# The last row tile's products in two half banks, and the first output-gate load behind the rows

## The chip, the cores and the metric

One core of a Trainium2 chip runs the kernel. The metric is the device time of one execution in microseconds, the median of several executions. The engines are named as in the profile: PE (TensorE, matrix products; PEld is its weight load), DVE (VectorE), ACT (ScalarE), POOL (GpSimd) and SP (SyncE, which here issues most of the DMAs). An engine works through its own instructions in order, and semaphores tie the engines together.

## The reference, cut to what matters

One decoder layer over 16 learned meta tokens and 1,024 rows of width 1,024, all in float32:

```python
u = rmsnorm(h, mix_norm_pre)
q, f_logit, i_in, g_out, v_pool, gate_a, gate_b = split(u @ w_in)
a = hgrn2(q, f_logit, i_in, g_out, ...)      # gated recurrence, 4 heads of 128
p = multiscale_pool(v_pool, pool_proj, pool_scale)
z = sigmoid(gate_a) * (a @ w_branch_hgrn) + sigmoid(gate_b) * (p @ w_branch_pool)
h = h + rmsnorm(z @ w_out, mix_norm_post)
u = rmsnorm(h, ffn_norm_pre)
gt = causal_dwconv(u @ ffn_w_gate, ffn_conv_w, ffn_conv_b)
y = (gelu(gt) * (u @ ffn_w_up)) @ ffn_w_down     # inner width 2,816
h = h + rmsnorm(y, ffn_norm_post)
return h[:, 16:]
```

`rmsnorm` divides each row by the root of its mean square and multiplies by a gain. The change touches three places: the loads at the very start (for the first `u @ w_in`), two scratch tiles in `hgrn2`, and the last product with its norm and row sum.

## The kernel before

**Precision.** Each float32 operand is split into a high and a low part of the type that PE multiplies at full rate, and a product is three: high by high, high by low, low by high (`mm3`, lines 187 to 190). So one block of 128 rows, one step of k and 512 columns is three matmuls of 512 columns into one PSUM bank (2 KB per partition, 512 floats; there are eight).

**The start.** `load_row` (line 451) issues the DMA of a tile of 128 rows on SP; `load_wi` (line 457) those of the weights of the value projection. In the text the order is: row tile 0, the gain, value weights 0, row tile 1, value weights 1 to 3, the other row tiles, small parameters. Then come, in an order written out by hand for PE, ACT and DVE (`manual_schedule`): 14 warm-up products of the identity (`warm`), the norm of a row tile (square on ACT with a sum per row, root, reciprocal and scaling on DVE), its transposes on PE into `pt` (line 431), the split into `uhi` and `ulo` (lines 434 and 436), the split of the value weights (lines 516 and 517), and the products `pv`. SP and POOL are not in that list. Their instructions, like all instructions outside such blocks, are ordered by a planner at build time, which lets an instruction go ahead as soon as what it needs is there. `Loader` (line 168) issues the DMAs of the next weights and their split through `wsplit` (line 149; its DMA is line 151, its cast line 154, its subtraction 155). At the end of the value projection a `Loader` is made for the first two output-gate projections ("G", line 1106), the first user of its buffers.

**The heads.** `head_steps` (line 646) runs one head of the recurrence in pieces that alternate with other products. It takes two scratch tiles: `sc` (128 by 1,024, the score matrix, zeroed by POOL at line 657) and `near` (128 by 256, the scores close to the diagonal, zeroed at line 658, two buffers for four heads). The products of six levels are written into them: into `near` by a predicated copy on DVE (line 720), into `sc` by plain copies (line 714); at the end `near` is copied into `sc` (line 777).

**The tail.** The last product of the layer is computed by a scheme with seven products of half size instead of eight (Strassen's), over four row tiles of 128 (NT = 4) in each half of the rows and 512 columns in each half of the columns. Its partial results stand in the SBUF tiles `c11`, `c12`, `c21` and `c22` (arrays named `acc` in the profile). Three of its stages run with both halves, eight banks at a time (`pa`, `pb`); `leave` adds them to the tiles. The last stage, from line 1759 on, has four banks, one for each tile. Over five steps of k (6 to 10) the products of all four tiles alternate with finishing the lower half of the rows; then each of the four upper tiles gets its last six steps of k and is finished:

- line 1777: DVE subtracts `c11` from the bank,
- `half_norm` (line 1699): ACT squares the 512 columns with a sum per row (1701), DVE multiplies them in place by the gain `g4` (1702),
- `finish` (line 1706): ACT takes the root (1708), DVE the reciprocal (1710) and, for each half of the columns, product and row sum (1714), and SP stores it (1715).

The right half of the columns, `c12`, has been through `half_norm` by then. `prep_last` splits operands for the last two steps of k. The order of the tail's instructions from line 1759 on is the planner's.

Of the kernel before, what the change touches and what calls it, by code (L numbers as in the profile page):

```python
# [11 lines left out]
AF = mybir.ActivationFunctionType  # L12
# [30 lines left out]
KT = 6  # L43
# [28 lines left out]
def trunk_kernel(ctx: ExitStack, tc: tile.TileContext, x, meta_tokens, mix_norm_pre,  # L72
# [35 lines left out]
    def bank(name="ps"):  # L108
        return stage["ps", "p"].tile([P, 512], F32, tag="ps", name=nm(name))
# [341 lines left out]
    def load_row(t0, rows):  # L451
        row = slot(D, name="row")
        src = meta_tokens[:, :] if t0 == 0 else x[0, t0 - NM : t0 - NM + rows, :]
        nc.sync.dma_start(row[:rows], src)
        return row

    def load_wi(j):
        raw = slot(1024, name="wiraw")
# [187 lines left out]
    def head_steps(h):  # L646
# [8 lines left out]
        near = small([P, NCH * SB], "near", "near", 2)  # L655
        n3 = near.rearrange("p (c t) -> p c t", c=NCH)
        pool_e.memset(sc, 0.0)
        pool_e.memset(near, 0.0)

        def over(t):  # L660
            return t[:, :NM].rearrange("p (o t) -> p o t", o=1).to_broadcast([P, HALO, NM])
# [254 lines left out]
    def job(kind, i):  # L916
        if kind == "F":
            return (wblock(WIN, 0, KD, CF + i * P, P), KD, u_all, CH_ALL, lambda r: post_f(i, r))
        if kind == "Q":
            return (wblock(WIN, 0, KD, CQ + i * P, P), KD, u_q, CH_Q, lambda r: post_q(i, r))  # L920
        if kind == "G":
            return (wblock(WIN, 0, KD, CG + i * P, P), KD, u_q, CH_Q, lambda r: post_g(i, r))
        if kind == "PV":
            return (wblock(WIN, 0, KD, CV + i * P, P), KD, u_all, CH_ALL, lambda r: post_pv(i, r))
        if kind == "PP":
            return (pool_proj[0, i].rearrange("(k c) d -> c k d", k=1), 1,
                    lambda k, lo, n: (pin[i][0][:, lo : lo + n], pin[i][1][:, lo : lo + n]), CH_Q,
                    lambda r: post_pp(i, r))
        if kind == "BA":
            return (wblock(w_branch_hgrn[0], 0, HEADS, i * P, P), HEADS, a_x, CH_Q, lambda r: post_branch(sas, i, r))  # L930
        return (wblock(w_branch_pool[0], 0, HEADS, i * P, P), HEADS, p_x, CH_Q, lambda r: post_branch(sbs, i, r))
# [122 lines left out]
    with tc.manual_schedule(engines={E.Activation, E.DVE, E.PE}):  # L1054
        warm(14)
        n0, n1 = (norm_steps(rows_in[i], P, g1) for i in range(2))
        next(n0)
        next(n0)
        un0 = next(n0)
        f0 = feature_steps(un0, P, uhi, ulo, vtiles[0][0])  # L1060
        split_wi(raws[0])
        next(f0)
        next(f0)
        next(f0)
        next(n1)
        next(f0)
        next(n1)
        un1 = next(n1)
        v_mm(vb[0], vtiles[0][0], 0)
        v_mm(vb[0], vtiles[0][0], 1)  # L1070
        split_wi(raws[1])
        f1 = feature_steps(un1, P, uhi, ulo, vtiles[1][0])
        next(f1)
        next(f1)
        split_wi(raws[2])
        next(f1)
        next(f1)
        split_wi(raws[3])
        for i, j in ((0, 1), (1, 0), (0, 2), (1, 1), (0, 3), (1, 2), (1, 3)):
            for k in (2 * j, 2 * j + 1):  # L1080
                v_mm(vb[i], vtiles[i][0], k)
        v_norm(2)
        v_norm(3)
        for i in range(2):
            v_feat(2 + i)
            v_norm(4 + i)
        for i in range(2):
            v_out(vb[i], vtiles[i][0])
        for i in range(2, len(vtiles)):
            ps = bank("pv")  # L1090
            for k in range(KD):
                v_mm(ps, vtiles[i][0], k)
            if i < 5:
                v_feat(i + 2)
            if i == 5:
                v_feat(7)
                v_feat(8)
            v_norm(i + 4)
            if i == 3:
                params()  # L1100
            if i == 5:
                for q in ("t2", "t1", "t3", "t4"):
                    two_halves(gq, q)
                sums = [gate_steps(d) for d in ds]
            if i == len(vtiles) - 1:
                gl = Loader([job("G", h)[:2] + (P,) for h in range(EARLY_G)])
            for j in SUMS_AT.get(i, ()):
                next(sums[j], None)
            v_out(ps, vtiles[i][0])
        gates.load_first(0)  # L1110
        gates.load_first(1)
        gates.ahead(2)
        for h in range(EARLY_G):
            src, n_k, xs, chunks, post = job("G", h)
            r = proj(None, 0, n_k, xs, chunks, ws=gl.next(), name="pg", by_bank=2 * h)
            if h == EARLY_G - 1:
                post(r)
            for j in SUMS_AT.get(9 + 2 * h, ()):
                next(sums[j], None)
            if h < EARLY_G - 1:  # L1120
                post(r)
            if h == 0:
                dve.tensor_tensor(vm_hl[:NM], vm_hl[:NM], vm_low[:NM], ALU.add)
                nc.sync.dma_start(vmd, vm_hl[:NM])
                gates.load_first(2)
                gates.ahead(4)
            for j in SUMS_AT.get(10 + 2 * h, ()):
                next(sums[j], None)

        close_pool("ps")  # L1130
        open_pool("pf", 4, PSUM)
        gates.load_first(3)
        for e in range(0, EARLY, 2):
            p = gates.start_pair(e)
            for f in [f[i] for i in range(2) for f in p]:
                f()
                for j in SUMS_AT.get(13, ()) if e == 0 else ():
                    next(sums[j], None)
# [532 lines left out]
    def prep_last(k, hold):  # L1671

        load_ops(3, k)
        if hold:
            hi, lo = slot(1024, F32R, "yh"), slot(1024, F32R, "yl")
        else:
            i = next_rot()
            hi, lo = big[1][:, i, :], big[1][:, 2 + i, :]
        cut(hi, lo, loads.pop((3, k)))
        held[k] = (hi[:, :512], lo[:, :512]), (hi[:, 512:], lo[:, 512:])  # L1680
# [76 lines left out]


    banks = [bank("pd") for _ in range(NT)]
    for n, k in enumerate(range(KT, KH)):  # L1760
        if n == 0:
            prep_last(KH - 2, False)
            for t in range(NT):
                dve.tensor_tensor(c12[t], c12[t], pb[t], ALU.add)
            prep_last(KH - 1, False)
        multiply(banks, held.pop(k), n == 0, False)
        if n < NT:
            half_norm(c22[n], NT + n, 1)
            half_norm(c21[n], NT + n, 0)
            finish(NT + n, c21[n], c22[n])  # L1770
            load_h(n)
        if n > 0:
            half_norm(c12[n - 1], n - 1, 1)
    for t in range(NT):
        for j in range(KT):
            multiply(banks, held[j], False, j == KT - 1, [t])
        dve.tensor_tensor(c11[t], banks[t], c11[t], ALU.subtract)
        half_norm(c11[t], t, 0)
        finish(t, c11[t], c12[t])
    close_pool("ps", "sm", "fm")  # L1780


# [27 lines left out]
```

## Time and profile before

| | us |
|---|---|
| time, median of 3 runs | 1331.35 (1329.1 to 1331.79) |
| the profiled execution | 1331.5 |
| its span, from the first instruction to the last | 1329.8 |
| PE busy | 1302.7 |
| DVE, ACT, POOL busy | 968.0, 572.9, 438.5 |

In the profile a line such as "L1777 DVE TENSOR_TENSOR acc<-pd,acc 128x512" is one instruction or a group: line of the program, engine, operation, what it writes and what it reads. A view in order of time begins with the start and the duration in us; brackets tell how long the engine stood idle before it and what ended that. Durations of one engine's instructions overlap somewhat, since an instruction starts while the one ahead is still writing. PE's matmuls overlap more: each is shown with its whole passage, and the pace is the distance of their starts. In a view of groups come the count, the total in us and the mean in ns. "SPq" marks the issue of a DMA; the data land later.

### The profile page before, as it was taken

The numbers are of one execution on the slowest core, as the hardware profiler recorded it, in microseconds if no ns is written. First come the engines' busy times: TensorE is split into PE (matmuls) and PEld (weight loads), VectorE is DVE, ScalarE is ACT, GpSimd is POOL, SyncE is SP. The second block draws the span as 40 slices with busy tenths as digits, with TensorE's granted clock in tenths as the row PEclk, the third lists the DMA queues.
The fourth block names the chain that finished last, engine by engine and source line by source line (L and its number), as shares of the span: only waits on it lengthen the run. The fifth ranks groups of instructions, "written<-read, shape, count | busy, mean of one in ns | idle before, by whom it ended". The sixth has DMA issues, their size and how long they took to land.

```text
span 1329.8 us, 21860 instructions
## 1 busy us (share of the span) xinstructions
PE 1302.7 (98%) x8665; PEld 1159.9 (87%) x8665; DVE 968.0 (73%) x1229; ACT 572.9 (43%) x962; POOL 438.5 (33%) x333
## 2 busy tenths in 40 slices
PE   8999999998899999999999999999999999999997
PEld 6799899998898999987899888888888888888886
DVE  5765655379967767766678999888999895455757
ACT  5553333366666665235564222322222233444443
POOL 2015331226624710051025555545555652000000
PEclk9999999998998999999999999999999999999999
DMA  7134533321011157987686777676766799666644
GB/s 260 53 105 145 134 111 104 108 69 49 19 52 36 35 175 263 337 287 253 229 291 231 192 207 193 196 206 164 181 157 141 183 237 318 216 224 222 222 174 158
DMA packets 139832, 230.56 MB, mean 173 GB/s; under 512 B 9080, under 2 KB 77340, under 8 KB 139730
## 3 DMA queue, kind: packets, MB, share of 16 engines
q1 hardware_dynamic: 127666, 204.78, 45.9%
q0 software_dynamic: 12064, 24.38, 11.1%
q8 instruction: 68, 1.11, 0.3%
q14 instruction: 34, 0.28, 0.1%
HBM read 165.59 MB, written 86.57 MB: 190 GB/s over the span
## 4 chain that ended last, share of the span: by engine, by line
PE 91%; DVE 3%; ACT 2%; DMA 2%; issue 1%; POOL 1%; SPq 0%; DVEq 0%; ACTq 0%
PE P L311 15%; PE P L312 15%; PE P L314 15%; PE pd L188 5%; PE pd L190 5%; PE pd L189 5%; PE pm L188 2%; PE pm L190 2%; PE pm L189 2%; PE ppv L208 1%; PE ppv L212 1%; PE ppv L209 1%; PE pbb L208 1%; PE pbb L209 1%; PE pbb L212 1%; PE pv L189 1%
## 5 line engine op out<-in xcount | busy, mean ns | idle before, releaser
L312 PE MATMUL P<-v,whi 128*128 128x512 f32 (+2 forms) x408 | 140.7, 353 | 0.0
L311 PE MATMUL P<-v,whi 128*128 128x512 f32 (+2 forms) x408 | 140.7, 352 | 0.0
L314 PE MATMUL P<-v,wlo 128*128 128x512 f32 (+2 forms) x424 | 135.1, 349 | 0.0
L1544 DVE TENSOR_TENSOR rot<-wraw,rot 128x1024 fp32r<-128x1024 f32 x31 | 37.9, 1224 | 72.3 <-ACT rot L1543 72.3
L282 POOL TENSOR_TENSOR swa<-wraw,wraw 128x512 f32<-128x512 f32 x28 | 43.4, 1549 | 138.9 <-DMA wraw<-in_ffn_w_gate_dram 73.9
L311 PEld LDWEIGHTS P<-v,whi 128*128 128x128 f32 x408 | 76.7, 188 | 10.5
L312 PEld LDWEIGHTS P<-v,whi 128*128 128x128 f32 x408 | 76.6, 188 | 10.2
L314 PEld LDWEIGHTS P<-v,wlo 128*128 128x128 f32 x424 | 74.0, 188 | 10.8
L256 ACT CAST whi<-wraw 128x512 fp32r<-128x512 f32 x78 | 46.1, 617 | 86.5 <-PE P L312 63.0
L190 PE MATMUL pd<-rot 128*128 128x512 f32 x272 | 82.1, 389 | 0.0
L189 PE MATMUL pd<-rot 128*128 128x512 f32 x272 | 82.1, 389 | 0.0
L188 PE MATMUL pd<-rot 128*128 128x512 f32 x272 | 81.1, 389 | 0.1
L1543 ACT CAST rot<-wraw 128x1024 fp32r<-128x1024 f32 x31 | 32.7, 1054 | 90.8 <-PE pd L190 89.4
L257 DVE TENSOR_TENSOR wlo<-wraw,whi 128x512 fp32r<-128x512 f32 x74 | 65.9, 912 | 2.8 <-ACT whi L256 2.7
L256 ACT CAST whi<-swa 128x512 fp32r<-128x512 f32 x56 | 33.4, 619 | 79.2 <-PE P L312 76.4
L1472 DVE SCALAR_TENSOR_TENSOR y<-g,par,y 128x1024 f32<-128x1024 f32 x44 | 65.6, 1491 | 0.8
L257 DVE TENSOR_TENSOR wlo<-swb,whi 128x512 fp32r<-128x512 f32 x56 | 61.4, 1102 | 6.0 <-ACT whi L256 6.0
L256 ACT CAST whi<-swb 128x512 fp32r<-128x512 f32 x56 | 33.4, 619 | 69.8 <-PE P L312 65.4
L188 PEld LDWEIGHTS pd<-rot 128*128 128x128 f32 x272 | 51.1, 188 | 11.1 <-DVE p L1480 0.5
L189 PEld LDWEIGHTS pd<-rot 128*128 128x128 f32 x272 | 51.0, 188 | 10.6
L190 PEld LDWEIGHTS pd<-rot 128*128 128x128 f32 x272 | 51.0, 188 | 10.6
L311 PE MATMUL P<-t4h,whi 128*128 128x258 f32 (+1 forms) x196 | 57.0, 307 | 0.0
(426 smaller groups left out, 4096.0 us busy)
## 6 DMA issues: line engine op xcount, KB each, us to landing
wraw<-in_w_in_dram SPq DMA_DIRECT2D x36, 512.0 KB, 5.1
yt<-ysum SPq DMA_DIRECT2D x33, 512.0 KB, 5.4
wraw<-in_ffn_w_gate_dram SPq DMA_DIRECT2D x26, 512.0 KB, 6.4
wraw<-in_ffn_w_up_dram SPq DMA_DIRECT2D x22, 512.0 KB, 5.9
wsum<-in_ffn_w_down_dram SPq DMA_DIRECT2D x22, 512.0 KB, 9.1
wraw<-in_w_out_dram SPq DMA_DIRECT2D x18, 512.0 KB, 4.8
ysum<-ys SPq DMA_DIRECT2D x11, 768.0 KB, 6.8
sa<-sscr SPq DMA_DIRECT2D x16, 513.0 KB, 6.4
```

The lines of the kernel that those rows point to most:

```text
L188: pe.matmul(ps, ahi, bhi, start=first, stop=False)
L189: pe.matmul(ps, ahi, blo, start=False, stop=False)
L190: pe.matmul(ps, alo, bhi, start=False, stop=last)
L256: act.copy(hi, src)
L257: (pool_e if 4 <= i < 2 * self.early else dve).tensor_tensor(lo, src, rr(hi), ALU.subtract)
L282: pool_e.tensor_tensor(s1, a21, a22, ALU.add)
L311: pe.matmul(d, whi[:, k, :], xh[:, c : c + w], start=(k == 0 and onto is None), stop=False, **go)
L312: pe.matmul(d, whi[:, k, :], xl[:, c : c + w], start=False, stop=False, **go)
L314: pe.matmul(x[:, o : o + w], wlo[:, k, :], xh[:, c : c + w], start=False, stop=(k == 3), **go)
L1472: dve.scalar_tensor_tensor(a, g[:, j : j + SEQ], cvw[:, j, m : m + 1], a, ALU.mult, ALU.add)
L1543: act.copy(hi, src)
L1544: dve.tensor_tensor(lo, src, rr(hi), ALU.subtract)
```

## The change

Three edits.

- The DMAs of the first two output-gate weights are queued on SP behind the DMA of the last row tile (`issue_after`: order of issue alone, with no wait for landing).
- `near` is no longer zeroed by a memset. It is copied on POOL from the first 256 columns of `sc`, just zeroed. So it can't run ahead of that memset, whose tile comes free later.
- In the last stage the fourth row tile's products are made in two pieces of 256 columns, in two banks: the one that it had, and a fifth (a bank that `pb` used; the addition of `pb[0]` to `c12[0]` is written ahead of `prep_last` for that). After the other three tiles are finished, the left piece gets its last six steps of k, then the right one. Each piece is subtracted, squared and multiplied by the gain on its own, the product into a new tile `left` and not in place; the left piece's sum of squares is added to the bias of the root by one small DVE instruction. Then `finish` follows as before.

```diff
     def load_row(t0, rows):
         row = slot(D, name="row")
         src = meta_tokens[:, :] if t0 == 0 else x[0, t0 - NM : t0 - NM + rows, :]
-        nc.sync.dma_start(row[:rows], src)
+        loaded_row.append(nc.sync.dma_start(row[:rows], src))
         return row
+
+    loaded_row = []
...
         pool_e.memset(sc, 0.0)
-        pool_e.memset(near, 0.0)
+        pool_e.tensor_copy(near, sc[:, : NCH * SB])
...
             if i == len(vtiles) - 1:
-                gl = Loader([job("G", h)[:2] + (P,) for h in range(EARLY_G)])
+                with tc.issue_after(loaded_row[-1].ins):
+                    gl = Loader([job("G", h)[:2] + (P,) for h in range(EARLY_G)])
...
     banks = [bank("pd") for _ in range(NT)]
+    pieces = [(banks[-1], slice(0, 256)), (bank("pd"), slice(256, 512))]
+
+    def multiply_pieces(ops, first, last, which=pieces):
+        (yh, yl), (wh, wl) = ops
+        tt = slice((NT - 1) * P, NT * P)
+        for ps, n in which:
+            mm3(ps[:, :256], (yh[:, tt], yl[:, tt]), (wh[:, n], wl[:, n]), first, last)
+
     for n, k in enumerate(range(KT, KH)):
         if n == 0:
+            dve.tensor_tensor(c12[0], c12[0], pb[0], ALU.add)
             prep_last(KH - 2, False)
-            for t in range(NT):
+            for t in range(1, NT):
                 dve.tensor_tensor(c12[t], c12[t], pb[t], ALU.add)
             prep_last(KH - 1, False)
-        multiply(banks, held.pop(k), n == 0, False)
+        ops = held.pop(k)
+        multiply(banks, ops, n == 0, False, range(NT - 1))
+        multiply_pieces(ops, n == 0, False)
...
-    for t in range(NT):
+    for t in range(NT - 1):
         for j in range(KT):
             multiply(banks, held[j], False, j == KT - 1, [t])
         dve.tensor_tensor(c11[t], banks[t], c11[t], ALU.subtract)
         half_norm(c11[t], t, 0)
         finish(t, c11[t], c12[t])
+    t = NT - 1
+    left = slot(512, name="left")
+    sums4 = small([P, 1], "sums4", "mq", 6)
+    for i in range(2):
+        ps, n = pieces[i]
+        for j in range(KT):
+            multiply_pieces(held[j], False, j == KT - 1, pieces[i : i + 1])
+        dve.tensor_tensor(c11[t][:, n], ps[:, :256], c11[t][:, n], ALU.subtract)
+        act.activation(junk[:, n], c11[t][:, n], AF.Square, accum_out=ssq4[:, 0, t : t + 1] if i else sums4)
+        dve.tensor_tensor(left[:, n], c11[t][:, n], g4[:, n], ALU.mult)
+        if i == 0:
+            dve.scalar_tensor_tensor(ssq4[:, 1, t : t + 1], sums4, 1.0 / D, ssq4[:, 1, t : t + 1],
+                                     ALU.mult, ALU.add)
+    finish(t, left, c12[t])
```

## The prediction

> **What bounds the kernel now.** I read the page first, then the busy time of each engine in five stretches, then the two ends in order of time, because the first view says that only the ends and one stretch in the middle have anything to give.
>
> ```profile
> span 1329.8 us, 21860 instructions
> ...
> PE 91%; DVE 3%; ACT 2%; DMA 2%; issue 1%; POOL 1%; SPq 0%; DVEq 0%; ACTq 0%
> ```
>
> ```profile
> 0.00:17.00 17.00, 11.37 (x52) 9.36 (x53) 7.04 (x12) 8.78 (x14) 9.54 (x40) 0.90 0.87 325
> 17.00:280.00 263.00, 263.00 (x1661) 241.84 (x1660) 151.80 (x243) 112.28 (x217) 61.68 (x43) 1.00 0.37 112
> 280.00:580.00 300.00, 285.62 (x3154) 278.01 (x3153) 228.52 (x299) 170.62 (x281) 108.41 (x57) 0.97 0.37 120
> 580.00:1323.00 743.00, 742.68 (x3803) 630.73 (x3801) 577.94 (x673) 280.22 (x448) 258.84 (x193) 1.00 0.72 213
> 1323.00:1330.00 7.00, 0.00 (x0) 0.00 (x0) 2.67 (x5) 1.02 (x3) 0.00 (x0) 0.78 0.35 130
> ```
>
> After the stretch come its length and the busy time of PE, PEld, DVE, ACT and POOL; the last three numbers are the granted clock, the DMA share and GB/s. TensorE (PE) is never idle from 17 to 280, and for 0.32 us from 580 to 1323. So a microsecond saved before 17 us arrives whole at 280. The recurrence of the four heads (280 to 580) has 14.4 us of PE idle time, and after 1323 PE has nothing left. The profiled execution took 1331.5 us, 1.7 over its span; the median of the runs shown is 1331.35, so what I take off one is taken off the other.
>
> **The start: the gate load goes behind the rows.** SP's queue, then ACT's instructions in order of time, and the point where PE begins to run without a pause (chain of waits):
>
> ```profile
> 0.81 0.44 SPq L151 DMA_DIRECT2D wraw<-in_w_in_dram  x1
> 1.30 0.57 SPq L454 DMA_DIRECT2D row<-in_x_dram  x1
> ...
> 2.38 0.43 SPq L459 DMA_DIRECT2D wiraw<-in_w_in_dram  x1
> ```
>
> ```profile
> 6.85 1.06 ACT L415 ACTIVATE un<-row 128x1024 f32<-128x1024 f32 x1 [4.56 <-DMA row<-in_x_dram]
> ...
> 9.48 1.05 ACT L516 CAST whi<-wiraw 128x1024 fp32r<-128x1024 f32 x1 [1.15 <-DMA wiraw<-in_w_in_dram]
> 10.58 0.59 ACT L434 CAST uhi<-pt 128x512 fp32r<-128x512 f32 x1
> 11.44 0.59 ACT L434 CAST uhi<-pt 128x512 fp32r<-128x512 f32 x1 [0.27 <-PE pt L431]
> 11.92 1.06 ACT L415 ACTIVATE un<-row 128x1024 f32<-128x1024 f32 x1
> ```
>
> ```profile
> 16.69 0.50 PE pv L189
> ```
>
> ACT stands in program order here and waits for two transfers: the first row tile (until 6.85) and the first value weights (until 9.48). From 9.48 to 16.69 it is compute behind compute. The gate load L151 was issued first. What it took of the transfers:
>
> ```profile
> DMA packets 930, 0.49 MB, mean 111 GB/s; under 512 B 4, under 2 KB 926, under 8 KB 930
> ```
>
> ```profile
> 2.00:4.40 2.40, 2.37 (x11) 2.38 (x12) 0.00 (x0) 0.28 (x2) 2.40 (x11) 1.00 0.71 199
> 4.40:6.90 2.50, 2.50 (x17) 2.50 (x17) 0.00 (x0) 0.05 (x1) 2.50 (x9) 1.00 1.01 389
> 6.90:9.50 2.60, 0.43 (x5) 0.27 (x4) 1.10 (x3) 1.42 (x4) 2.60 (x12) 0.98 1.03 410
> ```
>
> The first fence is the DMA view for 0 to 4.4 us. 930 packets and 0.49 MB are packets of some 0.5 KB, which is the gate load's 128 float columns; a row's packets are larger. So up to 4.4 us almost nothing but the gate load (512 KB, 0.52 MB) moved, and the first row came behind it. What its removal is worth to the transfer of L516 has two bounds. If the slow opening (199 GB/s from 2.0 to 4.4) belongs to any first transfer, the queue merely has 0.52 MB less ahead: 0.52 / 0.410 = 1.3 us. If it belongs to this load, the row starts where the load started: 4.4 - 2.0 = 2.4 us. A load of the same kind later decides which end is nearer:
>
> ```profile
> 83.00:84.40 1.40, 1.40 (x11) 1.40 (x11) 1.40 (x3) 1.40 (x5) 0.00 (x0) 1.00 0.86 331
> ```
>
> Here a gate load of the same 128-column form and a store share the engines, at 331 GB/s. The form is not slow by itself, so I stay near the lower end: **1.5 us**. The Trainium skill ("DMA: Bandwidth & Descriptors", Specifications) puts the least transfer for line rate at 512 B, which speaks in the same way against the large gain. By that rule alone the term would be the lower bound, 1.3.
>
> ACT gains a little more than that. L434's second copy waited 0.27 for the transposes, and the first began 1.10 after L516 with the second only 0.86 later, where 0.48 (11.44 to 11.92) is the pace without a wait. With the row earlier still than the weights, the transposes are done before ACT comes to them: 0.86 - 0.48 = 0.38. Everything to 16.69 hangs on ACT from there, so PE's unbroken run begins 1.5 + 0.38 = **1.9 us earlier**, bounds 1.7 and 2.8; below both, 0.5 (1.30 - 0.81) if only the issue slot is won.
>
> The load that is moved is read late:
>
> ```profile
> L154 ACT CAST whi<-wraw x2: 1056/1056/1057, 64.9 to 66.3; 128x1024 fp32r<-128x1024 f32 x2
> ```
>
> Both gate loads now queue on SP after the last row, perhaps ahead of five small parameter loads, which are read after four row tiles; the gate weights are cast only from 64.9 us on. Cost 0; were the cover gone, one 512 KB transfer, 1.3.
>
> **`near` is copied from the zeroed `sc`.** POOL's instructions, and the DVE group that first reads the third head's tile:
>
> ```profile
> 1.08 0.56 POOL L658 MEMSET near<- 128x256 f32 x2
> ...
> 289.68 0.95 POOL L657 MEMSET sc<- 128x1024 f32 x1
> ...
> 355.43 0.32 POOL L658 MEMSET near<- 128x256 f32 x1
> ```
>
> ```profile
> 358.93 0.42 DVE L720 COPY_PREDICATED near<-mask,sl 128x128 f32<-128x128 uint8 x1
> ```
>
> Two memsets leave the start, so the identity, and with it PE's warm-up products, come up to 0.6 us earlier; they end before the transposes either way, so 0. The copies now follow each head's memset of `sc`. No POOL copy of this size and type is in the trace: between the memset's 0.32 and 0.95 (four times the columns) I take 0.4. Four of them make 1.6 us of POOL work, two of them new to the heads' stretch, where POOL is busy 108 of 300 us. Charged on the path: 0. This stretch is ordered by a planner, and an order that changes is a rival below.
>
> **The tail.** The last products and what follows, then PE's pace from the chain of waits (first and last of 26 pieces):
>
> ```profile
> 1321.01 1.41 DVE L1714 SCALAR_TENSOR_TENSOR hrow<-acc,rstd,hrow 128x512 f32<-128x512 f32 x2
> ...
> 1322.38 0.39 PE L190 MATMUL pd<-yh,yl 128*128 128x512 f32 x1
> 1322.80 0.69 DVE L1777 TENSOR_TENSOR acc<-pd,acc 128x512 f32<-128x512 f32 x1 [0.39 <-PE pd L190]
> 1323.53 0.63 ACT L1701 ACTIVATE junk<-acc 128x512 f32<-128x512 f32 x1 [3.03 <-DVE acc L1777]
> ...
> 1324.28 0.69 DVE L1702 TENSOR_TENSOR acc<-acc,g 128x512 f32<-128x512 f32 x1 [0.79 <-ACT junk L1701]
> 1324.28 0.29 ACT L1708 ACTIVATE std<-ssq 128x1 f32<-128x1 f32 x1
> 1324.89 0.16 DVE L1710 RECIPROCAL rstd<-std 128x1 f32<-128x1 f32 x1
> 1325.08 1.41 DVE L1714 SCALAR_TENSOR_TENSOR hrow<-acc,rstd,hrow 128x512 f32<-128x512 f32 x2
> ```
>
> ```profile
> 1316.87 0.23 PE pd L189
> ...
> 1322.54 0.24 PE pd L190
> ```
>
> Half-width forms are in the trace: products of 256 and 258 columns (24 of them between these two starts), and DVE and ACT over 256.
>
> ```profile
> 713.01 0.28 PE L311 MATMUL P<-t2h,whi 128*128 128x258 f32 x1
> ...
> 715.85 0.39 PE L311 MATMUL P<-v,whi 128*128 128x512 f32 x1
> ```
>
> ```profile
> L402 DVE TENSOR_TENSOR t2l<-tt,t2h 128x256 fp32r<-128x256 f32 x16 | 6.0, 418 | 2.3 <-ACT t2h L401 2.3
> ...
> L401 ACT CAST t2h<-tt 128x256 fp32r<-128x256 f32 x16 | 5.7, 411 | 4.0 <-DVE tt L1321 4.0
> ```
>
> Added on PE: a full product takes (1322.54 - 1316.87) / 25 = 0.227, a half one (715.85 - 713.01) / 24 = 0.118. One split costs 2 x 0.118 - 0.227 = 0.010. There are 11 steps of k (five, then six) with 3 products each for the last tile, so 33 splits: **+0.33**, all on the path. The Trainium skill ("TensorE: Matmul & The Clock Gate", Back-to-back issue gap) gives N / 2.4 + 2.5 ns, by which a split would cost 2.5 ns and the lot an estimated 0.08; the measured rows stand.
>
> Removed, from L1777 to the last L1714, 1325.08 - 1322.80 = 2.28 us: L1777 at half width, 0.69 to 0.42 (-0.27); the square likewise, 0.63 to 0.41 (-0.22); and the gain product L1702 no longer holds the reciprocal. It ran in place, so it started only when ACT had read the tile, and the reciprocal came at 1324.89. Now it writes another tile beside the square, and the reciprocal follows the root's end, 1324.57, by about 0.04 (-0.28). Sum -0.77. The left half's subtraction, product and small sum (about 1.0 us of DVE) lie beside the right half's 18 products (18 x 0.118 = 2.1 us), but DVE also has tile 2's two row operations there, 1.41 from 1321.01. 2.4 of 2.1 us does not quite fit, and if the planner puts the left half last, the right half's subtraction waits some 0.35. I charge 0.1. Tail: 0.33 - 0.77 + 0.10 = **-0.34**, bounds -0.44 and -0.1. The fifth bank is the first of `pb`, free after one addition that now stands ahead of the operand preparation; PE has three other tiles' products meanwhile, so 0; uncovered it would be that addition, about 0.7.
>
> **Sum:** -1.9 - 0.3 = **-2.2 us**: 1331.5 becomes 1329.3, and the median 1331.35 becomes **1329.1**. About 0.2%, 2.66 us, is what a measurement of this kernel can tell from no change, so the line for faster is 1328.69.
>
> **The rivals.**
> *The opening was the gate load's own.* Then the start gives 2.4 + 0.38 = 2.8, with the tail 3.1: 1328.2. For it speaks that the DMA share rises from 0.71 to 1.01 just when the gate load ends; against it the later load of its form at 331 GB/s.
> *The gain at the start is only the issue slot.* The first row meets the slow opening in full and its larger packets do not shorten it: 0.5 + 0.3 = 0.8, giving 1330.5. Against it: 0.52 MB less stand ahead of L516's transfer.
> *The copies are queued badly and it gets slower.* The third head's `near` became free at 355.43 and DVE wanted it at 358.93: 3.5 us of room, minus 0.4. A copy put behind two POOL operations of some 2 us holds DVE, in whose order everything behind L720 then waits, and PE in this stretch waits for DVE. This decides as soon as the stalls exceed the 2.2 us won; with all four heads losing 2 us each it is +8 - 2.2 = +5.8, so 1337. Against it: POOL is idle two thirds of the stretch, and `sc` is zeroed early enough for heads one and two.
> *The planner's new order is better.* Up to 14.4 us of idle time lie there; a gain of 2 gives 1327.
> *The change doesn't do what it says:* the left half falls wholly behind the right. The tail is then +0.33 - 0.28, about 0, and the time 1329.5, inside the forecast.
>
> **How the numbers follow.** Forecast (1328.4 to 1329.8) 0.50, of which 0.13 lies below 1328.69; opening 0.20; issue slot 0.15; bad queue 0.08; better order 0.07. Faster 0.13 + 0.20 + 0.07 = 0.40, within 0.37 + 0.15 = 0.52, slower 0.08. The range takes in the two start rivals with their spread and part of the better order: 1326.8 to 1331.2.
>
> **What would show it.** First row square at about 5 instead of 6.85; L516 at about 8.0; PE's unbroken run from about 14.8. Last product some 0.33 later relative to the run's start; 1.5 us instead of 2.28 from the last subtraction to the row operation. PE idle between 280 and 580 still about 14.4. Wrong if that idle time moves by more than 1, or if L516 still waits past 9.

## The result, and the profile after

The changed kernel takes 1327.82 us (median of 20 runs, 1325.73 to 1329.80) beside 1331.17 for the kernel before (20 runs): a ratio of 0.9975, with an interval of 0.9967 to 0.9983, or 3.35 us less. Measured again beside other runs it was 1326.98 against 1330.48, a ratio of 0.9976 (0.9967 to 0.9984). The forecast was 1329.1. Three executions below, two of the kernel before at over 1,430 us and one of the tail alone at 2147.5 us, ran at a mean granted clock of 0.85 and 0.56 and are left out of all ratios and averages, and of the tail's median.

**The start.** SP's queue and ACT's instructions in order of time, then PE's first product of the unbroken run (chain of waits):

```profile
0.81 0.38 SPq L454 DMA_DIRECT2D row<-in_x_dram  x1
1.25 0.42 SPq L145 DMA_DIRECT2D g<-in_mix_norm_pre_dram  x1
1.70 0.43 SPq L461 DMA_DIRECT2D wiraw<-in_w_in_dram  x1
```

```profile
4.28 1.06 ACT L415 ACTIVATE un<-row 128x1024 f32<-128x1024 f32 x1 [1.98 <-DMA row<-in_x_dram]
...
8.01 1.04 ACT L518 CAST whi<-wiraw 128x1024 fp32r<-128x1024 f32 x1 [2.26 <-DMA wiraw<-in_w_in_dram]
8.96 1.07 ACT L434 CAST uhi<-pt 128x512 fp32r<-128x512 f32 x2
```

```profile
14.70 0.50 PE pv L189
```

The row is there at 4.28 instead of 6.85, the value weights at 8.01 instead of 9.48. The two casts after that follow without a pause, and PE's run begins at 14.70 instead of 16.69. The same three stretches of the windows view as before (PE, PEld, DVE, ACT and POOL busy, granted clock, that is PE's clock as a share of full speed, DMA share, GB/s):

```profile
2.00:4.40 2.40, 2.40 (x13) 2.40 (x13) 0.00 (x0) 0.41 (x3) 2.40 (x9) 1.00 0.94 307
4.40:6.90 2.50, 2.50 (x15) 2.50 (x14) 0.47 (x2) 1.32 (x3) 2.50 (x10) 1.00 0.97 290
6.90:9.50 2.60, 1.67 (x12) 1.08 (x11) 1.84 (x3) 1.49 (x3) 2.60 (x9) 1.00 1.03 410
```

The first stretch now runs at 307 GB/s instead of 199; the second has dropped from 389 to 290 at nearly full share. Between the row and the value weights stands the gain's load (second in SP's queue). Thus the row gained 2.57 us and the weights 1.47. Over both stretches together the two kernels moved the same: 1.45 MB before and 1.46 after. The row is early because it comes first; the weights, because 0.52 MB less stands ahead of them.

The transposes gained too. PE, kernel before and changed kernel:

```profile
9.46 1.94 PE L431 MATMUL pt<-ident,un 128*128 128x128 f32 x8 [2.17 <-DVE un L420]
```

```profile
7.81 1.23 PE L431 MATMUL pt<-ident,un 128*128 128x128 f32 x8 [0.47 <-DVE un L420]
```

In the kernel before, PE waited 2.17 us for the row's norm after its warm-up products, and the granted clock was 0.50 from 9.40 to 12.82, so the eight transposes took 1.94 us. In the changed kernel they ran at a clock of 1.00.

**The heads.** The windows of 280 to 580 us:

```profile
280.00:580.00 300.00, 287.49 (x3163) 279.43 (x3162) 230.98 (x303) 171.94 (x284) 110.80 (x59) 0.97 0.38 125
```

PE is busy 287.49 us and not 285.62, so its idle time is 12.5 us and not 14.4. That alone says little: a second profile of the same kernel ("again" below) has 13.7, and the tail edit alone, which changes nothing here, has 12.8. What differs in each profile with the edit is a place at the third head's `near`. First the kernel before, then the changed one; POOL, DVE and PE in order of time:

```profile
355.43 0.32 POOL L658 MEMSET near<- 128x256 f32 x1
355.70 2.04 POOL L754 TENSOR_TENSOR q<-q,e 128x512 f32<-128x512 f32 x1
...
356.63 1.66 DVE L755 TENSOR_TENSOR kk<-kk,e 128x512 f32<-128x512 f32 x1
358.32 0.68 DVE L714 COPY sc<-sl 64x512 f32<-64x512 f32 x1
...
359.06 0.94 PE L790 MATMUL ds<-vh,kt 128*128 128x128 f32 x6 [1.00 <-DVE sc L714]
```

```profile
353.76 1.41 POOL L660 COPY near<-sc 128x256 f32<-128x256 f32 x1
355.13 1.73 POOL L756 TENSOR_TENSOR q<-q,e 128x512 f32<-128x512 f32 x1
...
354.95 0.77 DVE L757 TENSOR_TENSOR kk<-kk,e 128x512 f32<-128x512 f32 x1
355.74 0.68 DVE L716 COPY sc<-sl 64x512 f32<-64x512 f32 x1
...
356.48 0.94 PE L792 MATMUL ds<-vh,kt 128*128 128x128 f32 x6 [0.32 <-DVE sc L716]
```

The copy takes 1.41 us where the memset took 0.32, so POOL's product `q<-q,e` starts later against what DVE does. Before, it started 0.93 us ahead of DVE's product `kk<-kk,e`, which took 1.66 and ended 0.55 after it. Now DVE's product starts first, 0.18 ahead, and takes 0.77, although the two still overlap by 0.58. DVE's copy out of a PSUM bank, and PE, which waits for that bank, come 0.9 us sooner after that product's start (355.74 - 354.95 instead of 358.32 - 356.63), and PE's wait in these two profiles is 0.32 instead of 1.00. In other profiles PE comes to this place earlier or later, and its wait differs; the 0.9 doesn't.

**The tail.** The last products, then DVE and ACT:

```profile
1317.32 0.28 PE L190 MATMUL pd<-yh,yl 128*128 128x256 f32 x1
...
1318.87 1.42 DVE L1717 SCALAR_TENSOR_TENSOR hrow<-acc,rstd,hrow 128x512 f32<-128x512 f32 x2
...
1319.12 0.28 PE L190 MATMUL pd<-yh,yl 128*128 128x256 f32 x1
...
1320.20 0.42 DVE L1801 TENSOR_TENSOR acc<-pd,acc 128x256 f32<-128x256 f32 x1
...
1321.53 0.16 DVE L1713 RECIPROCAL rstd<-std 128x1 f32<-128x1 f32 x1 [0.44 <-ACT std L1711]
1321.73 0.75 DVE L1717 SCALAR_TENSOR_TENSOR hrow<-left,rstd,hrow 128x512 f32<-128x512 f32 x1
```

From the subtraction to the row operation it is 1.53 us (1321.73 - 1320.20) instead of 2.28, as forecast. But the subtraction starts 1.08 after the last product's start, where it was 0.42 before (1322.80 - 1322.38): DVE is still at tile 2's two row operations (1318.87). And the products go at a pace of 0.120 ((1319.12 - 1317.32) / 15), so a split costs 0.013 and 33 splits 0.43. DVE was late because the planner had put the subtraction of tile 1 ahead of the gain product of tile 0:

```profile
1311.05 0.69 DVE L1791 TENSOR_TENSOR acc<-pd,acc 128x512 f32<-128x512 f32 x1 [2.24 <-PE pd L190]
1311.65 0.68 DVE L1705 TENSOR_TENSOR acc<-acc,g 128x512 f32<-128x512 f32 x1
```

2.24 us of DVE pass idle there, and the work held back never catches up before the end.

### The profile page after: what moved, and what is told of

Its sections match the earlier page's. It is cut to its first block, busy times and chain, and to the rows that moved or that the text cites. A ratio compares the mean times of both kernels' runs of the same rounds, so it can differ in the third digit from the quotient of the medians.

```text
span 1326.4 us, 21933 instructions
## 1 busy us (share of the span) xinstructions
PE 1302.8 (98%) x8698; PEld 1161.1 (88%) x8698; DVE 970.2 (73%) x1232; ACT 572.7 (43%) x964; POOL 441.8 (33%) x333
## 4 chain that ended last, share of the span: by engine, by line
PE 90%; DVE 4%; ACT 3%; DMA 2%; issue 1%; SPq 0%; DVEq 0%; ACTq 0%
PE P L311 15%; PE P L312 15%; PE P L314 15%; PE pd L188 5%; PE pd L189 5%; PE pd L190 5%; PE pm L188 2%; PE pm L190 2%; PE pm L189 2%; PE ppv L208 1%; PE ppv L212 1%; PE ppv L209 1%; PE pbb L208 1%; PE pbb L209 1%; PE pbb L212 1%
```

## The experiments

All times are medians in us; the ratio is to the kernel before, run beside them.

| kernel | time | before | ratio (95%) |
|---|---|---|---|
| changed kernel | 1327.82 | 1331.17 | 0.9975 (0.9967 to 0.9983) |
| changed kernel, again | 1326.98 | 1330.48 | 0.9976 (0.9967 to 0.9984) |
| gate loads only | 1328.67 | 1330.26 | 0.9986 (0.9977 to 0.9995) |
| gate loads only, again | 1329.49 | 1330.29 | 0.9998 (0.9988 to 1.0008) |
| near only | 1329.60 | 1330.26 | 0.9996 (0.9986 to 1.0005) |
| tail only | 1330.66 | 1330.26 | 1.0008 (0.9999 to 1.0018) |
| gate loads and near | 1326.51 | 1330.48 | 0.9970 (0.9960 to 0.9979) |
| gate loads and near, again | 1327.16 | 1330.29 | 0.9983 (0.9973 to 0.9992) |
| gate loads and one idle POOL copy | 1327.36 | 1330.52 | 0.9976 (0.9963 to 0.9988) |
| changed kernel, tail ordered by hand | 1327.30 | 1330.26 | 0.9978 (0.9969 to 0.9987) |
| gate loads, near, gain product aside | 1326.82 | 1330.48 | 0.9975 (0.9964 to 0.9986) |
| the same, gain spread by PE | 1329.37 | 1330.48 | 0.9987 (0.9974 to 1.0000) |
| the same as the last but one, products in the waits | 1329.28 | 1330.29 | 0.9997 (0.9988 to 1.0006) |

The stages of the profiled executions, from the views of the tiles' instructions: the start of the first product into `pf` (first head), from there to the first into `pbb` (branch products), and from the first into `pd` to the end of the span.

| kernel | first pf | pf to pbb | pd to the end |
|---|---|---|---|
| before | 248.0 | 234.8 | 217.0 |
| changed; again | 246.1; 246.0 | 233.9; 233.1 | 217.5; 217.5 |
| gate loads only; again | 246.2; 246.3 | 235.0; 236.1 | 217.0; 217.0 |
| near only | 248.1 | 235.5 | 217.0 |
| tail only | 247.8 | 234.0 | 217.5 |
| gate loads and near; again | 245.9; 246.0 | 234.6; 233.1 | 217.0; 217.0 |
| gate loads and POOL copy | 246.2 | 232.0 | 217.0 |
| tail by hand | 246.0 | 232.5 | 217.0 |
| gain product aside | 246.1 | 232.3 | 216.7 |

The last column holds to 0.1 us for one and the same edit, and the first to 0.4. The middle one does not: it moves by over 1 us between two executions of the same kernel.

### Each part alone

The three edits of the change, each put into the kernel before by itself.

> Before, with only the two gate loads queued behind the rows. Both theories: the first row's square at about 4.3 us and PE's unbroken run from 14.7 (16.69 before). Theory A (three separate parts: the start by the moved load, the heads by the copies of near, a lost tail): the first pm product at 580.1 (582.1 before), 2.0 earlier and no more, time 1329.2. Theory B (what the heads gained is not the copies' doing, but comes with the earlier start or differs from one execution to the next): the first pm product anywhere from 578.2 to 580.1, time 1327.3 to 1329.2. If the near memsets on POOL had to leave the start first, the run would begin at 15.2 or later.

> Before, with near copied from sc instead of zeroed. POOL's order changes in eight rows, that of the other engines not at all. Theory A: PE's unbroken run from 16.7 as before, the last pq product 0.6 and the first pm product 1.0 to 2.0 earlier than in the run before (392.8 and 582.1), time 1329.2 to 1330.2. Theory B: both as before within 0.3, or moved by an amount that comes from elsewhere, time 1331.2.

> Before, with only the tail of the change. Start and heads as before. If the order of DVE is what costs (the second tile's subtraction queued ahead of the first tile's gain product), the right half's subtraction starts about 1.1 us after the last product's start (0.42 before), and the whole is 0.5 slower, 1331.7. If my forecast of the tail holds, 0.35 after the last product, and 0.3 faster, 1330.9.

The gate loads alone bring PE's first product of the heads 1.8 us forward (248.0 to 246.2) and 1.6 us in time. The tail alone is 0.5 longer in the profile, and 0.4 in time, within its interval. `near` alone gives 0.66, also within its interval. Together these make about -1.9, not -3.35. Each of these times is uncertain by some 1.2 us, so this gap alone proves nothing, but it was a reason to look on. The order of the instructions doesn't explain it: outside the tail, ACT, DVE and PE have the same order in all four kernels, and only SP's two rows and POOL's `near` rows differ.

### Two parts together, and the change again

> The changed kernel unaltered, for a second profile beside the next kernels. If the 2 us that its first profile showed between 260 and 582 us differ from execution to execution, the distance from the first pf to the first pbb product and from there to the first pm product (233.9 and 98.2 us then, 234.8 and 99.3 before) come out anywhere from 232 to 236 and 97 to 100. If they belong to the change, 233.9 and 98.2 within 0.3. Start and tail as in the first profile: run from 14.7, and 217.5 from the first pd product to the end.

> The changed kernel without its tail (before's tail). Both theories: run from 14.7; from the first pd product to the end 217.0 as before, so 0.5 less than the changed kernel. Theory A (the copies win 1 to 2 us in the heads): time 0.5 below the changed kernel's in this call. Theory B (they win nothing): the same 0.5 below, but both only 1.4 to 1.9 us below before.

Without the tail the time is 1326.51 beside 1326.98: the tail wins nothing, and the gain is that of the other two edits. Gate loads and `near` together bring 4.0 us where their sum was 2.2. To see whether `near` has a share, both kernels ran side by side once more:

> Only the gate loads behind the rows, again, beside start and near together. Theory: 1.9 to 2.0 us under the kernel before, as in its first run (1328.3 to 1328.6 beside 1330.3 to 1330.6).

> Gate loads behind the rows and near copied, the old tail, again. Theory (the third head's copy makes POOL's product of queries late, so DVE's product of keys no longer runs beside it and takes 0.77 instead of 1.66 us, which PE then waits less for): 0.7 us under the kernel with the gate loads alone, so 2.6 under the kernel before. Rival A (the copies are worth nothing to PE): the same as the gate loads alone. Rival B (the two edits help each other, as the 4.0 us of the first run says): 2 us under the gate loads alone.

1329.49 against 1327.16: `near` is worth 2.3 us on top of the gate loads. Over both rounds the 24 runs of the two edits average 2.1 us less than the 23 of the gate loads alone, with an interval of 1.3 to 2.9. That was rival B of that expectation in size; the 0.9 of DVE's product accounts for less than half.

### One useless copy on POOL

If the place in the fences above is all of it, `near` need not be touched. Gate loads behind the rows, `near` zeroed by memsets, and one added instruction:

```diff
-        eng(f"qsmul.{h}").tensor_tensor(qs[:, NM:], qs[:, NM:], q[:, NM:], ALU.mult)
+        late = eng(f"qsmul.{h}").tensor_tensor(qs[:, NM:], qs[:, NM:], q[:, NM:], ALU.mult)
+        if h == 1:
+            with tc.issue_after(late.ins):
+                late = pool_e.tensor_copy(qs[:, NM : NM + 256], qs[:, NM : NM + 256])
...
+        if h == 1:
+            with tc.issue_after(late.ins):
+                eng(f"e1q.{h}").tensor_tensor(q2, q2, e1[:, : SEQ // 2], ALU.mult)
```

> The gate loads behind the rows, near zeroed by memsets as before, and one useless instruction on POOL: it copies 128x256 of the second head's qs onto itself, right where the third head's near copy stood (ahead of the product of queries q<-q,e); no other instruction moves. Theory (all that the near edit is worth comes from this one place: the copy makes POOL's product late, so DVE's product of keys beside it takes 0.77 instead of 1.66 us, and PE's wait for the second group of state products gets shorter, and with it the chance that the clock falls there): the profile shows 0.77, and the time is that of gate loads and near together, a ratio of about 0.9977 to the kernel before (the two runs of that: 0.9970 and 0.9983). Rival A (the near edit's worth lies elsewhere): as the gate loads alone, about 0.9992 (0.9986 and 0.9998). Rival B (only the 0.8 us of DVE counts, not the clock): about 0.9986.

The ratio is 0.9976. POOL, DVE and PE in order of time:

```profile
353.85 1.16 POOL L752 COPY qs<-qs 128x256 f32<-128x256 f32 x1
354.98 1.73 POOL L761 TENSOR_TENSOR q<-q,e 128x512 f32<-128x512 f32 x1
...
354.79 0.77 DVE L764 TENSOR_TENSOR kk<-kk,e 128x512 f32<-128x512 f32 x1
355.59 0.68 DVE L716 COPY sc<-sl 64x512 f32<-64x512 f32 x1
...
356.33 0.94 PE L799 MATMUL ds<-vh,kt 128*128 128x128 f32 x6 [1.61 <-DVE sc L716]
```

An instruction that does nothing, in that one place, is worth as much as the whole `near` edit, as far as the runs can tell: its 12 runs average 1.9 us less than the 23 with the gate loads alone (interval 0.9 to 2.8). So, on top of the gate loads, the edit's gain is not in what is no longer zeroed, nor in the other three copies: it is that POOL's product starts later than DVE's. The kernel with gate loads alone shows 1.66 and 1.67 for DVE's product in its two profiles; every profile with `near` or with this copy shows 0.77. Wherever PE waits for that bank, it goes on 1.53 or 1.54 us after the start of DVE's product with the edit or the copy, and 2.43 or 2.44 without.

Two things don't fit. PE's wait itself is not shorter here: 1.61, since PE came early. And `near` alone, without the gate loads, has the same 0.77 and 1.53 and yet gained only 0.66, within its interval. So the 2 us belong to this place together with the gate loads, and why they need both is open.

### The tail, by hand and without halves

The order of ACT and DVE in the last loop written out by hand, so that DVE finishes tile 0 before tile 1 and takes the left half between tile 2's two row operations:

```diff
+    with tc.manual_schedule(engines={E.Activation, E.DVE}):
...
+        t = NT - 1
+        piece(0, t)
+        store(t - 1, 0, c11[t - 1], rstd)
...
+        store(t - 1, 1, c12[t - 1], rstd)
+        piece(1, t)
+        finish(t, left, c12[t])
```

> The changed kernel, with DVE's and ACT's order in the last loop written by hand: tile by tile, and the left half's subtraction and gain product ahead of the third tile's two row operations. If DVE's order costs the tail, the right half's subtraction starts 0.35 to 0.5 after the last product's start instead of 1.08, and the kernel is 0.6 to 0.7 faster than the changed one, 1327.1. Rival (DVE simply has too much to do in the right half's 2.1 us): still 0.8 or more after it, time as the changed kernel, 1327.8.

```profile
1317.26 0.28 PE L190 MATMUL pd<-yh,yl 128*128 128x256 f32 x1
...
1317.92 0.42 DVE L1807 TENSOR_TENSOR acc<-pd,acc 128x256 f32<-128x256 f32 x1
```

The subtraction comes 0.66 after the last product's start and not 1.08, and the stage is 217.0: the planner's order cost 0.4 to 0.5. But that is no more than the kernel before had, so the halves only pay for themselves even so. What is left of the idea without them is the gain product into another tile, at full width:

```diff
-        dve.tensor_tensor(src, src, g4[:, j * 512 : (j + 1) * 512], ALU.mult)
+        dve.tensor_tensor(src if dst is None else dst, src, g4[:, j * 512 : (j + 1) * 512], ALU.mult)
```

> As the one ahead, but the last tile's gain product is written to another tile (whole width, one bank, no halving). If the reciprocal's wait for the product in place was a cost by itself, 0.28 comes off the tail without any halving: 216.7 from the first pd product to the end, 0.8 less than the changed kernel. Rival (the reciprocal waits for the product in DVE's order anyway): 217.0.

```profile
1317.39 0.69 DVE L1780 TENSOR_TENSOR acc<-pd,acc 128x512 f32<-128x512 f32 x1 [0.38 <-PE pd L190]
1318.12 0.69 DVE L1705 TENSOR_TENSOR left<-acc,g 128x512 f32<-128x512 f32 x1
1319.20 0.16 DVE L1713 RECIPROCAL rstd<-std 128x1 f32<-128x1 f32 x1 [0.39 <-ACT std L1711]
1319.40 0.75 DVE L1717 SCALAR_TENSOR_TENSOR hrow<-left,rstd,hrow 128x512 f32<-128x512 f32 x1
```

From the subtraction to the row operation 2.01 instead of 2.28: the 0.28 of the forecast's third removed term, alone and free. The stage is 216.7, the shortest of the table's; in time 0.3 is below what these runs can tell.

### The gain's load at the start

The gain is one row of 4 KB (1,024 floats), loaded to all 128 partitions. To see what its load costs, one row of it was loaded and PE spread it with products of ones:

```diff
+    nc.sync.dma_start(grow[:1], mix_norm_pre[0:1, :])
...
+            pe.matmul(gb, onesm[:1], grow[:1, n], start=True, stop=True)
+            dve.tensor_scalar(g1[:, n], gb, float(P), None, ALU.mult)
```

> As the one ahead, but the pre-norm gain is no longer loaded 128 times over (512 KB): one row of 4 KB is loaded and spread over the partitions by PE and DVE. Theory: the changed kernel's slow stretch of transfers from 4.4 to 6.9 (290 GB/s at a DMA share of 0.97) belongs to that load, which stands ahead of the value weights; without it L516's cast starts at 6.0 to 6.8 instead of 8.0 and PE's run at 13.0 to 13.7. Rival (any transfer opens slowly and the weights land no earlier than 7.5, or the transposes wait for the warm-up products until 7.4): the run starts at 14.0 or later.

```profile
11.67 1.66 PE L431 MATMUL pt<-ident,un 128*128 128x128 f32 x8
```

```profile
5.81 1.04 ACT L519 CAST whi<-wiraw 128x1024 fp32r<-128x1024 f32 x1
12.77 1.18 ACT L434 CAST uhi<-pt 128x512 fp32r<-128x512 f32 x2 [5.91 <-PE pt L431]
```

The cast of the value weights waits for no DMA any more and starts at 5.81, 2.2 us sooner than in the changed kernel. So the gain's load, 512 KB ahead of the weights, does hold them back by at least that. But PE's broadcast products and a second batch of warm-up products behind them kept the transposes until 11.67, and `uhi` came at 12.77 instead of 8.96: the way taken cost more than the load.

### The clock in the heads

Why should 0.9 us on DVE be worth 2? The second theory came from the granted clock. After three or four waits in the heads, in most profiles, it falls to half, each time for one or two stretches of 3.41 us that follow one another without regard to the instructions. Here are four such stretches of the changed kernel's second profile (PE busy first, granted clock third from the end):

```profile
307.74:311.15 3.41, 1.43 (x96) 1.27 (x96) 3.41 (x4) 3.37 (x9) 3.41 (x2) 1.00 0.02 5
311.15:314.56 3.41, 1.44 (x14) 1.47 (x15) 3.32 (x3) 1.67 (x2) 1.27 (x1) 0.50 0.25 75
314.56:317.97 3.41, 3.41 (x15) 3.29 (x14) 3.40 (x3) 3.06 (x5) 3.12 (x3) 0.50 0.72 217
317.97:321.38 3.41, 3.41 (x23) 3.41 (x23) 3.33 (x6) 0.00 (x0) 2.19 (x1) 1.00 0.05 15
```

A stretch in which PE is busy for 1.4 of 3.41 us is followed by one at half clock, a full one by one at full clock. In other executions the same borders lie elsewhere against the kernel's start, so the same wait costs PE nothing, 1.7 us (half of 3.41) or up to twice that. The Trainium skill ("TensorE: Matmul & The Clock Gate", What's actually happening) describes such a window of 3413 ns that runs on its own; the trace agrees in the length. The page lets the clock fall after a whole idle window; here 1.4 us of work in one didn't prevent it.

If so, products that nothing reads, put into the waits, must hold the clock up. 31 of them were added to the kernel with the gain product aside, with the orders of all engines held to what they were:

```diff
+            if h == 0 and lv >= SB:
+                fill(ps[:, :P], 6 if lv == SB else 7, onesm, seen[-1][:, NM : NM + P])
+            if (h, lv) == (3, 4):
+                fill(ps[:, :P], 8, onesm, seen[-1][:, NM : NM + P])
...
+        if h == 0:
+            fill(ps[:, :P], 10, onesm, kd[:, NM : NM + P])
```

> The start and the near edit, the old tail with the last tile's gain product written aside, and 31 products whose results nothing reads, put on PE ahead of four waits in the heads' stretch (6 and 7 before the last two level products of the first head, 10 before its diagonal blocks, 8 before the fourth head's second level); the other engines' orders and PE's own are those of the run with the gain product aside. Theory (the spread from one execution to the next, and 6 to 7 us of every execution, come from the granted clock falling to 0.5 for 3.41 us at a time after these waits): the granted clock stays at 1.00 through the heads, the time that it costs there falls from 5.8 to 7.6 us in the profiles so far to under 2, the time from 1326.8 to about 1322, and the runs of this kernel lie closer together than the 6 us of the kernel before. Rival (the clock follows something else than PE's pauses): the clock falls as often as before, and the time is 1326.8 or up to 1 us later, since the extra products stand in the way.

The mean granted clock of its 11 runs is 0.996 or 0.997 in each, where the kernel before lies between 0.989 and 0.995. The same place in its profile:

```profile
307.74:311.15 3.41, 3.06 (x109) 2.86 (x110) 3.41 (x4) 3.37 (x9) 3.41 (x2) 1.00 0.02 5
311.15:314.56 3.41, 3.10 (x32) 2.82 (x33) 3.31 (x3) 1.65 (x2) 1.28 (x1) 1.00 0.22 65
```

So it is PE's waits that make the clock fall: where they were filled, it stayed up. The rest of the theory fell: the kernel is no faster than the one before, and 2.5 slower than the one it was built from. What PE won here it lost at the next wait, since the engines it waits for were no earlier. Shown first is the wait of the kernel without the added products, then that with them:

```profile
344.20 0.76 PE L775 MATMUL sb<-q,kk 128*32 128x32 f32 x64 [2.63 <-POOL kk L757]
```

```profile
341.20 1.80 PE L775 MATMUL pt<-ident,kd 128*128 128x128 f32 x8 [2.89 <-ACT d L690]
342.79 0.42 PE L778 MATMUL pt<-ident,kd 128*16 128x128 f32 x1
343.19 3.23 PE L697 MATMUL sb<-kd,onesm 128*128 128x128 f32 x20
346.34 0.73 PE L788 MATMUL sb<-q,kk 128*32 128x32 f32 x62
```

PE came early to the transposes, waited 2.89 us for `kd` there, ahead of the added products and not where they stood; the clock fell (0.50 from 341.37 to 344.78), and the ten products (20 records) took 3.23 us, half of it at half clock, in the way of what was ready. Its profiled execution took 1326.48, the fastest of its runs; where the other 2.8 us of the median go can't be read from it, and stays open.

The clock does have a part in the spread. Of 110 runs of the kernel before, those with a mean clock of 0.991 or less (35) averaged 1331.6 us, those with 0.993 or more (61) 1329.7. And the 23 runs with the gate loads alone have a mean clock of 0.9930, the 48 with `near`, the POOL copy or the whole change on top 0.9940. Over PE's 1302 us that is 1.3 us, and with DVE's 0.9 it makes the 2.2 us measured. That PE, going on sooner at this place, is spared some of the falls would fit these numbers: both profiles of the gate loads alone show a fall there. But so do that of `near` alone and one of the two edits together, and the POOL copy's shows none after a wait of 1.61. The 12 runs of `near` alone have a mean clock of 0.9914, not above the 0.9924 of the kernel before beside them. So the share of the clock is worked out from means and not shown by an experiment of its own.

## Why the prediction was right, and where it was not

The time lies inside the range and on the side of faster, to which the forecast gave 0.40. It lies below the 1328.4 to 1329.8 that had its half: 1.2 us of the 3.35 were not in its sum of 2.2, and two of its three terms were off in opposite directions. So the total is in part luck.

- **Start, -1.9.** The path was right, and so was the size in the profile: 1.99 sooner (16.69 to 14.70). The transfer of the first value weights gained 1.47 of the 1.5 taken, and ACT's second copy lost its wait. But the row that decided for 1.5 was misread. From 83.00 to 84.40 no gate load moved, but a store alone; its packets are of 4 KB, where those of the gate load are of some 0.5 KB:

```profile
DMA packets 113, 0.46 MB, mean 331 GB/s; under 512 B 0, under 2 KB 0, under 8 KB 113
```

The next load of 128 columns, issued at 83.66, came behind it, at 130 GB/s from 84.40 to 88.00. Only where such loads fill the engines (235 to 236, 639 packets of 512 B and nothing else) do they reach 327. So the choice of the lower end was luck. It held, because both kernels moved the same bytes up to 6.90, and 0.52 MB less ahead at 410 GB/s is 1.3. And the wait for the transposes, 0.38 of the term, was read as their lateness alone; they also ran at half clock, 1.94 instead of 1.23. In time the edit alone gave 1.6 and 0.8, not 1.9. 1.7 to 1.8 are still there when the heads begin (246.2 and 246.3 instead of 248.0); the heads of its two profiles took 0.1 and 1.3 longer than before. Why is open.
- **`near`, 0.** This is the step that failed: "Charged on the path: 0". The copies were costed at 0.4 each, and only harm was looked for. Two copies added 0.2 each to a DVE instruction beside them, and the third took 1.41, since DVE was busy. That delay, which the rival "queued badly" priced as a loss, let DVE's product start ahead of POOL's and, together with the gate loads, gave about 2 us. The forecast named its own test, an idle time between 280 and 580 that moves by more than 1. It moved by 1.9 in the first profile and by 0.7 in the second, and by up to 1.4 between two profiles of one kernel, so the test decides nothing; the runs with and without the edit do.
- **Tail, -0.34.** Wrong in sign: +0.5 in every profile that has it as the planner ordered it. The removed terms were right (1.53 from subtraction to row operation, 1.5 forecast). The splits cost 0.43 and not 0.33 (0.120 a half product, not 0.118). And "I charge 0.1" for DVE's crowding was too small: the subtraction came 0.66 later after the last product's start than before. The working had seen that 2.4 us of DVE work don't fit into 2.1; it had not seen that the planner could start the backlog 8 us earlier, by putting one subtraction ahead of a gain product.
- **The rivals.** "The planner's new order is better" has the size of what happened (1327), but not the cause: no order changed outside the tail. "The opening was the gate load's own" (1328.2) lies nearer to the time than the forecast too, but PE's run began 1.99 sooner and not 2.8.

## What to carry to other kernels

When an edit moves an instruction on one engine, look at what runs beside it on the engine that shares its way to memory, before and after: here a slower POOL instruction was worth 2 us, beside the gate loads, because it changed which of two products started first. And before a row of a view is taken as evidence on one transfer, look at the packets in that stretch. Before halving the last tile's work, check whether the engine that finishes it has room; the free part of the idea, a result written to another tile so that the reciprocal needn't wait, needs no halving. A wait that is shortened on PE alone comes back at the next wait, when another engine sets the pace.

## What the runs showed of the hardware

- Two products of 128x512 floats, one on DVE and one on POOL, took 1.66 and 2.04 us when POOL's started 0.93 ahead, and 0.77 and 1.73 when DVE's started 0.18 ahead. With POOL idle, the same DVE product took 0.69 (at 422.12 in the kernel before). In each profile the one that starts second ends a fixed time after the first: 0.55 for DVE's, 1.15 for POOL's. That they take turns, in the order of their starts, fits this; no run tried other distances. A DVE instruction may take over twice its time, and the profile shows it as busy and not as waiting. The Trainium skill ("GPSIMD Engine Reference", Key points) says that POOL shares its SBUF interfaces with VectorE and contends with DVE instructions that have two SBUF inputs; this is such an instruction, and the trace agrees.
- From 2.00 to 6.90 us the DMA engines moved 1.45 MB in the kernel before, 1.46 in the changed one and 1.60 without the gain's full load, though the order and the size of the packets differ; in the first two 410 GB/s came only after 6.90. The gain's load is not slow in itself: in the kernel before it moved behind the row, in stretches of 389 and 410 GB/s. Loads in packets of 512 B reached 327 GB/s where they filled the engines.
- The granted clock halves for 3.41 us at a time after some waits of 1.6 to 3.2 us on PE, on a grid that is not tied to the kernel's start. Runs of one kernel differ by 3 to 9 us in all; with 12 runs of each kernel, a difference of 2.1 us came out with an interval of 0.9 to 3.2.
